# State-space layer: chunks of 4 tokens become chunks of 8, with column strips on TensorE and taps spread in memory

## The chip, the cores and the metric

The program runs on one core of one Trainium2 chip. The metric is the device time of one execution in microseconds; of several runs the median is given. The engines named in the rows are PE (matrix products), DVE, ACT and POOL (operations on vectors), and SP, which here issues the transfers.

## What is computed

A trunk of two layers for 256 tokens, with 16 meta tokens put ahead (272 columns) and 2048 channels. Layer 0 mixes by attention and a short convolution, layer 1 by a diagonal complex state-space layer with a gated output (GLU). Each is followed by a SwiGLU feed-forward net, with norms between. The part that matters here is the state-space mixer: 128 groups of 16 channels, each group with 64 complex states.

```python
def s5_mixer(u, a_re, a_im, log_step, b_re, b_im, c_re, c_im, d_skip, w_glu1, w_glu2):
    ...
    lb_re = mag * jnp.cos(ang)
    lb_im = mag * jnp.sin(ang)
    ...
    bu_re = jnp.einsum('blgh,gph->blgp', ug, bb_re)
    bu_im = jnp.einsum('blgh,gph->blgp', ug, bb_im)
    ...
    _, _, x_re, x_im = lax.associative_scan(_complex_affine_combine, (a_r, a_i, bu_re, bu_im), axis=1)
    y = (jnp.einsum('blgp,ghp->blgh', x_re, c_re.astype(f32))
         - jnp.einsum('blgp,ghp->blgh', x_im, c_im.astype(f32)))
    y = y.reshape(Bsz, L, D_MODEL) + d_skip.astype(f32) * uf
    g = jax.nn.gelu(y).astype(u.dtype)
    return (g @ w_glu1) * jax.nn.sigmoid(g @ w_glu2)
```

## The kernel before

Activations lie with channels on partitions: 16 tiles of 128 channels (`KT`) by 272 tokens. Every large product is made of three (high by high, high by low, low by high part, L296 to L298, L754). A weight chunk (`raw`, 384 to 512 KB) comes by DMA into one of four buffers, ACT makes its high part (L101), DVE its low part (L108), then PE uses both. SP issues all transfers in the order of the program.

The state-space layer works in chunks of `T` tokens. From the state at the start of a chunk the outputs of all its tokens follow by a product with C times powers of the transition; the effect of inputs on outputs inside the chunk is a triangular product with kernel taps. So the scan runs over `NC` = 272/`T` columns only. The matrices for this depend on parameters alone. `par_tile(k)` computes them for channel tile k on POOL and DVE, with transposes and a few small products on PE (`kmat`, L1029, is the one for the taps), and stores them to memory (`scr`). It is cut into ticks; the function `tick()` runs one after each weight chunk, so that all 16 tiles are made beside the feed-forward net of layer 0 (about 515 to 1205 us). Small tables of parameters are set up in the same way a little earlier.

After that net the stage proper follows. The input is turned by a round trip through memory (`write_u`, `read_u`, L1241 to L1247), so that the tokens of a chunk lie on partitions, and scaled by `r_u`. Then `s5_step(i)` (L1276) runs for i = -1 to 17. Each step issues operations for several tiles, as the table `stages` says, with a lag in steps: loads, `f_u` (scale, DVE, tile m), `f_c` (drive x of the states, PE, L1145), `f_mod` (rotation on DVE into rc and rs_, then z on POOL), `f_scan` (two DVE scans, L1171, rotation back, then xp on POOL), `f_y` (output product, PE, L1185 and L1188, and an ACT copy yn), `f_yt` (four PE transposes, L1197, and an ACT copy yy, then the first GELU steps), `f_g1` (POOL), `f_g2` and `f_g3` (DVE and ACT; the results xh and xl are the high and low part of the GLU's input). Lines 811 and 814 are the helpers `tt` and `stt` that record most DVE operations. Steps 18 to 23 run in the ticks of the first GLU block, whose first product starts at 1439.09 us.

## Time and profile before

| what | value |
| --- | --- |
| median of 3 runs | 2399.0 us (2397.54 to 2399.22) |
| the profiled execution's own time | 2399.63 us |
| its span, first to last instruction | 2397.9 us |
| PE busy | 2341.3 us (98%) |
| DVE busy | 1431.2 us (60%) |
| ACT busy | 1062.3 us (44%) |
| POOL busy | 708.5 us (30%) |
| mean granted TensorE clock | 0.991 |
| DMA, mean over the span | 187 GB/s |

Busy shares are means over stages with different limits, so a stage has to be read by itself: in windows of busy time, in the chain of waits (the work that ended last, followed back), and in the timeline of an engine. One matmul call on 4-byte floats is two records in the trace; the calls that work on the high and low parts are one. Durations of neighbouring operations overlap a little, so the time from start to start is what counts.

### The profile page before, as it was taken

The page shows a single profiled execution, that of the slowest core. Times are in us where ns is not written, and L with a number is a line of the kernel's source. Part 1 is how long each engine was busy: PE and PEld are TensorE (multiplying, and loading weights), DVE is VectorE, ACT ScalarE, POOL GpSimd, SP SyncE. Part 2 cuts the span into 40 slices and gives each one's busy share as a digit, 9 for nine tenths or more (in the row PEclk, how much of TensorE's full clock was granted, in tenths as well). Part 3 has the DMA queues.
Part 4 walks back from the last instruction along what each step waited for, and adds up shares of the span by engine and source line. Part 5 has one row for each costly group of instructions (what it writes and reads, how often), then busy time and mean ns, then how long its engine had stood idle before and what let it go on. Part 6 is the DMA issues. An engine that isn't in the chain of part 4 may idle for free.

```text
span 2397.9 us, 45436 instructions
## 1 busy us (share of the span) xinstructions
PE 2341.3 (98%) x18006; PEld 2251.5 (94%) x18006; DVE 1431.2 (60%) x1977; ACT 1062.3 (44%) x1613; POOL 708.5 (30%) x1214
## 2 busy tenths in 40 slices
PE   8999999999999999999999879999999999999998
PEld 7999999999999999999999769998998899989996
DVE  6555555677654576656554896457564455645665
ACT  5434344554343344334344555446444444433443
POOL 2000001248775878567501462105000000000001
PEclk9999999999999999999999899999999999999999
DMA  6555555457876788777755755555666566656664
GB/s 173 142 158 144 157 149 170 138 173 192 222 220 196 204 229 213 216 202 205 212 188 175 263 208 165 185 170 150 198 186 205 183 183 178 204 185 185 189 189 158
DMA packets 392537, 447.35 MB, mean 187 GB/s; under 512 B 75476, under 2 KB 324084, under 8 KB 392180
## 3 DMA queue, kind: packets, MB, share of 16 engines
q1 hardware_dynamic: 392096, 444.37, 63.3%
q8 instruction: 141, 2.31, 0.4%
q14 instruction: 72, 0.59, 0.1%
q10 hardware_dynamic: 228, 0.08, 0.0%
HBM read 413.50 MB, written 30.87 MB: 185 GB/s over the span
## 4 chain that ended last, share of the span: by engine, by line
PE 88%; DVE 7%; POOL 2%; ACT 1%; issue 1%; DMA 1%; SPq 0%; DVEq 0%; POOLq 0%; ACTq 0%
PE mm L296 23%; PE mm L298 23%; PE mm L297 22%; PE mm L754 5%; PE mm L1379 3%; PE mm L1380 3%; PE mm L1378 3%; DVE v L1171 1%; DVE wlo L108 1%; PE mm L1029 1%; PE mm L1017 1%; DVE rc L811 0%; DVE m L811 0%; DVE yq L814 0%; DVE hn L709 0%
## 5 line engine op out<-in xcount | busy, mean ns | idle before, releaser
L108 DVE TENSOR_TENSOR wlo<-raw,whi 128x768 fp32r<-128x768 f32 (+2 forms) x891 | 938.8, 1065 | 508.5 <-ACT whi L101 503.9
L101 ACT CAST whi<-raw 128x768 fp32r<-128x768 f32 (+2 forms) x891 | 777.5, 887 | 791.0 <-PE mm L297 460.8
L296 PE MATMUL mm<-xh,whi 128*128 128x272 f32 (+1 forms) x3712 | 1067.1, 287 | 0.8 <-DVE m L811 0.6
L298 PE MATMUL mm<-xh,wlo 128*128 128x272 f32 (+1 forms) x3712 | 1063.5, 287 | 4.0 <-DVE wlo L108 3.5
L297 PE MATMUL mm<-xl,whi 128*128 128x272 f32 (+1 forms) x3712 | 1057.1, 285 | 2.2 <-DVE xl L718 2.1
L298 PEld LDWEIGHTS mm<-xh,wlo 128*128 128x128 f32 x3712 | 700.6, 189 | 7.7 <-DVE wlo L108 7.6
L296 PEld LDWEIGHTS mm<-xh,whi 128*128 128x128 f32 x3712 | 702.3, 189 | 4.2 <-ACT sq L308 0.8
L297 PEld LDWEIGHTS mm<-xl,whi 128*128 128x128 f32 x3712 | 700.7, 189 | 3.2 <-DVE xl L718 3.2
L296 PE MATMUL mm<-ah,whi 128*128 128x272 f32 x944 | 273.9, 290 | 0.5 <-ACT m L677 0.5
L298 PE MATMUL mm<-ah,wlo 128*128 128x272 f32 x944 | 273.3, 289 | 0.0
L297 PE MATMUL mm<-al,whi 128*128 128x272 f32 x944 | 271.6, 288 | 0.0
L811 POOL TENSOR_TENSOR m<-m,gb 128x512 f32<-128x512 f32 x8 | 12.1, 1513 | 709.2 <-ACT mm L1392 692.9
L296 PEld LDWEIGHTS mm<-ah,whi 128*128 128x128 f32 x944 | 177.6, 188 | 1.1 <-ACT m L677 0.7
L298 PEld LDWEIGHTS mm<-ah,wlo 128*128 128x128 f32 x944 | 177.9, 188 | 0.1
L297 PEld LDWEIGHTS mm<-al,whi 128*128 128x128 f32 x944 | 177.9, 188 | 0.0
L313 POOL TENSOR_TENSOR sqacc<-sqacc,sq 128x272 f32<-128x272 f32 (+1 forms) x81 | 84.7, 1045 | 242.5 <-ACT sq L308 240.7
L1379 PE MATMUL mm<-wlo,ah 128*128 128x512 f32 x352 | 137.2, 390 | 1.0 <-DVE wlo L108 1.0
L1378 PE MATMUL mm<-whi,ah 128*128 128x512 f32 x352 | 137.8, 392 | 0.0
L1380 PE MATMUL mm<-whi,al 128*128 128x512 f32 x352 | 137.1, 390 | 0.0
L763 DVE TENSOR_TENSOR gs<-mm,r 128x272 f32<-128x272 f32 (+1 forms) x88 | 38.2, 434 | 113.2 <-PE mm L298 113.2
L581 POOL TENSOR_TENSOR z<-c,x 128x272 f32<-128x272 f32 x8 | 6.3, 785 | 289.7 <-DVE x L574 192.8
L1379 PEld LDWEIGHTS mm<-wlo,ah 128*128 128x128 f32 x352 | 66.1, 188 | 15.3 <-DVE wlo L108 1.8
(424 smaller groups left out, 2503.8 us busy)
## 6 DMA issues: line engine op xcount, KB each, us to landing
raw<-in_ffn_w_gate_dram SPq DMA_DIRECT2D x224, 384.0 KB, 3.8
raw<-in_ffn_w_up_dram SPq DMA_DIRECT2D x224, 384.0 KB, 3.9
raw<-in_ffn_w_down_dram SPq DMA_DIRECT2D x168, 512.0 KB, 4.6
raw<-in_ab_w_in_dram SPq DMA_DIRECT2D x90, 512.0 KB, 3.9
raw<-in_s_w_glu_dram SPq DMA_DIRECT2D x64, 384.0 KB, 3.6
raw<-in_ab_w_o_dram SPq DMA_DIRECT2D x32, 512.0 KB, 4.2
w<-scr SPq DMA_DIRECT2D x16, 768.0 KB, 4.3
scr<-xw SPq DMA_DIRECT2D x16, 512.0 KB, 5.0
```

Of the source, the lines that this page charges most:

```text
L101: self.nc.scalar.copy(hi[:, :n], self.raw[i][:, :n])
L108: self.nc.vector.tensor_tensor(lo[:, :n], raw[:, :n], hi[:, :n].bitcast(F32), op=ALU.subtract)
L296: nc.tensor.matmul(ps, hi, bh, start=first, stop=False)
L297: nc.tensor.matmul(ps, hi, bl, start=False, stop=False)
L298: nc.tensor.matmul(ps, lo, bh, start=False, stop=last)
L313: eng.tensor_tensor(self.acc[:, :self.cols], self.acc[:, :self.cols], sq[:, :self.cols], op=ALU.add)
L754: nc.tensor.matmul(pss[o], w[:, k, o * P:(o + 1) * P], xx[:, k, :cols], start=(k == 0 and w is hi and xx is xh), stop=False)
L763: nc.vector.tensor_tensor(gs[:, o, :cols], pss[o], r["r"][:, :cols], op=ALU.mult)
L1017: nc.tensor.transpose(pt[:, j * P:(j + 1) * P], wide["b"][:, i, j].rearrange("p s h -> p (s h)"), ident)
L1378: nc.tensor.matmul(pss[a], ah[:, kt, ts_], hi[:, k], start=(kt == 0), stop=False)
L1379: nc.tensor.matmul(pss[a], ah[:, kt, ts_], lo[:, k], start=False, stop=False)
L1380: nc.tensor.matmul(pss[a], al[:, kt, ts_], hi[:, k], start=False, stop=(kt == kts - 1))
```

## The change

`T` goes from 4 to 8, so a scan has 34 columns per state row where it had 68. The powers are made by doubling: complex products with the first, second and fourth power for each of B and C; the last of C runs on DVE in two ticks. The matrices are no longer widened with zeros for pairs of groups: B's and C's products use half of the partitions, and PE is addressed in column strips (`f_c` two strips of 64, `f_y` and `kmat` four of 32, by where the output's partitions start). `f_y` delivers channels in blocks of 32 that one DVE transpose turns, straight from PSUM; the transposes on PE and both ACT copies are gone, and xh and xl are written with a stride of 8. The triangular matrix of taps is made in memory: `store_k` and `zeros` write the 16 x 15 x 128 block `taps`, one tile later `spread_k` copies it eight times into `toep`, whose rows are read back with a skew as `kt`, in one transfer per tile. `f_load1` is merged into `f_load`, and the loads of `w2` and `kt` go out two steps ahead.

```diff
-T = 4
+T = 8
...
+    ZB = 2 * T - 1
+    KL = (ZB + T - 1) * P
+    taps = [dram.tile([16, ZB, P], F32, name=f"taps{k}") for k in range(KT)]
+    toep = [dram.tile([T, 16 * KL + P], F32, name=f"toep{k}") for k in range(KT)]
...
-        def bpow(n):
-            cmul([bc[:, i, :, T - 1 - n] for i in range(2)], [bc[:, i, :, T - n] for i in range(2)], s["lbr"][:, q], s["lbi"][:, q], ct)
...
+        def bpow(e):
+
+            bc, n = wide["b"], 1 << e
+            ar, ai = powers(e)
+            cmul(steps(bc, T - 2 * n, n), steps(bc, T - n, n), ar[:, q], ai[:, q])
...
         def kmat():
-            pt = d["pk"] = bank()
+
+            d["pk"] = []
+            for g in range(2):
+                pt = bank()
+                d["pk"].append(pt)
+                r = slice(64 * g, 64 * g + 64)
+                for i in range(2):
+                    for j in range(4):
+                        nc.tensor.matmul(pt[32 * j:32 * j + 32, :P], wide["b"][r, i, j, T - 2:].rearrange("p n h -> p (n h)"),
+                                         wide["c"][r, i, j, :T].rearrange("p n h -> p (n h)"), start=(i == 0), stop=(i == 1))
...
+        def store_k():
             for j in range(4):
-                for i in range(2):
-                    nc.tensor.matmul(pt[:32, j * 64:(j + 1) * 64], wide["b"][:, i, j, T - 1], cc[:, i, j, :T].rearrange("p n h -> p (n h)"), start=(i == 0), stop=(i == 1))
-
-        def k_first():
-
-            v = d["pk"][:32, :256].rearrange("p (qn h) -> p qn h", h=16)
-            o = kz[:32].rearrange("p q n (g h) -> p (q n) g h", g=2)
-            sh = [32, 4 * T, 2, 16]
-            tt(o, v.unsqueeze(2).to_broadcast(sh), evn[:32].unsqueeze(1).unsqueeze(3).to_broadcast(sh), M_)
-            tt(kz[:32, :, 0], kz[:32, :, 0], d["dd"], A_)
-
-        def ke(t):
-            V.tensor_copy(kz[32 * t:32 * t + 32, :, t:, :], kz[:32, :, :T - t, :])
+                nc.sync.dma_start(out=taps[k][:, T - 1:, 32 * j:32 * j + 32], in_=kk[32 * j + 16:32 * j + 32].rearrange("p n g h -> p n (g h)"))
+
+        def zeros():
+            nc.sync.dma_start(out=taps[k][:, :T - 1], in_=kz.unsqueeze(1).to_broadcast([16, T - 1, P]))
+
+        def spread_k():
+            v = toep[k][:, :16 * KL].rearrange("t (h n) -> t h n", h=16)[:, :, :ZB * P]
+            nc.sync.dma_start(out=v, in_=taps[k].rearrange("h b n -> h (b n)").unsqueeze(0).to_broadcast([T, 16, ZB * P]))
...
         def store():
             w = scr[k]
-            nc.sync.dma_start(out=w[:, CW0:KW0], in_=wide["c"].rearrange("p i q n h -> p (i q n h)"))
-            nc.sync.dma_start(out=w[:, KW0:], in_=kz.rearrange("p q t h -> p (q t h)"))
-            for i in range(2):
-                nc.sync.dma_start(out=w[:, EW0 + NT * i:EW0 + NT * (i + 1)].rearrange("p (q c) -> p q c", q=4), in_=d["e"][:, i, :, :NC])
-
-        loads[k] = load
+            nc.sync.dma_start(out=w[:, EW0:CW0], in_=d["e"].rearrange("p i q c -> p (i q c)"))
+            nc.sync.dma_start(out=w[:, CW0:], in_=wide["c"].rearrange("p i q n h -> p (i q n h)"))
...
+            [lambda: cpow(1, 1, 2), zeros], [lambda: etab(0), lambda: k and spreads[k - 1]()], [lambda: xw(0), lambda: etab(1)], [lambda: xe(0), lambda: cpow(2, 1, 4, V, 0)],
+            [lambda: xw(1), lambda: cpow(2, 1, 4, V, 1)], [lambda: xe(1)],
+            [kmat, store_x], [], [k_first], [store_k, store]]
...
-        w = sp.tile([P, EW0], F32, tag="w", name="w", bufs=3)
-        nc.sync.dma_start(out=w, in_=scr[k][:, :EW0])
+        w = sp.tile([P, CW0], F32, tag="w", name="w", bufs=5)
+        nc.sync.dma_start(out=w, in_=scr[k][:, :CW0])
...
     def f_load2(k):
-        w = sp.tile([P, SCR - CW0], F32, tag="w2", name="w2", bufs=2)
+        w = sp.tile([P, SCR - CW0], F32, tag="w2", name="w2", bufs=3)
         nc.sync.dma_start(out=w, in_=scr[k][:, CW0:])
+        kt = td[k]["kt"] = sp.tile([P, T, 8, 16], F32, tag="kt", name="kt", bufs=3)
+        v = toep[k].rearrange("t n -> (t n)")[:P * KL].rearrange("(r n) -> r n", r=P)
+        nc.sync.dma_start(out=kt.rearrange("r t j h -> r (t j h)"), in_=v[:, (T - 1) * P:ZB * P])
...
         for i in range(2):
             for j in range(4):
-                c0 = XW0 + 512 * i + P * j
-                nc.tensor.matmul(d["x"][:, i, j * NC:(j + 1) * NC], d["w"][:, c0:c0 + P], d["U"][:, j], start=True, stop=True)
+                for g in range(2):
+                    c0, o = XW0 + 512 * i + P * j + 64 * g, i * QC + j * NC
+                    nc.tensor.matmul(d["x"][64 * g:64 * g + 64, o:o + NC], d["w"][:, c0:c0 + 64], d["U"][:, 2 * j + g], start=True, stop=True)
...
     def f_y(k):
         d = td[k]
-        ps = sps.tile([P, 512], F32, tag="y", name="y")
-        for j in range(4):
-            o = ps[:NC - CM, j * P:(j + 1) * P]
-            w = d["w2"]
-            nc.tensor.matmul(o, d["U"][:, j, CM:], w[:, KW0 - CW0 + P * j:KW0 - CW0 + P * (j + 1)], start=True, stop=False)
+        ps = d["ps"] = sps.tile([P, 2, 512], F32, tag="y", name="y")
+        wv = d["w2"].rearrange("p (a n) -> p a n", a=8)[:, :, 16:]
+        kv = d["kt"].rearrange("p t j h -> p j t h")
+        for g in range(2):
+            for j in range(4):
+                nc.tensor.matmul(ps[32 * j:32 * j + 32, g, :P].rearrange("c (t h) -> c t h", t=T), d["U"][:, 2 * j + g, CM:], kv[:, 2 * j + g], start=True, stop=False)
+        for g in range(2):
+            r = slice(64 * g, 64 * g + 64)
             for i in range(2):
-                c0 = 512 * i + P * j
-                nc.tensor.matmul(o, d["xp"][:, i, j, CM:], w[:, c0:c0 + P], start=False, stop=(i == 1))
-        d["yn"] = sp.tile([NC - CM, T, 4, 32], F32, tag="yn", name="yn", bufs=1)
-        nc.scalar.copy(d["yn"].rearrange("c t q h -> c q t h"), ps[:NC - CM].rearrange("c (q t h) -> c q t h", q=4, t=T))
+                for j in range(4):
+                    nc.tensor.matmul(ps[32 * j:32 * j + 32, g, :P], d["xp"][r, i, j, CM:], wv[r, 4 * i + j], start=False, stop=(i == 1))
     def f_yt(k):
         d = td[k]
-        pt = sps.tile([P, 512], F32, tag="yt", name="yt")
-        n = NC - CM
-        for t in range(T):
-            nc.tensor.transpose(pt[:, t * n:(t + 1) * n], d["yn"][:, t].rearrange("c q h -> c (q h)"), ident[:n, :n])
         y = d["y"] = sp.tile([P, NREAL], F32, tag="yy", name="yy")
-        nc.scalar.copy(y.rearrange("p (c t) -> p t c", t=T), pt[:, :NREAL].rearrange("p (t c) -> p t c", t=T))
+        V.transpose(y.rearrange("p (t g h) -> p t g h", t=T, g=2), d["ps"][:, :, :P].rearrange("p g (t h) -> p t g h", t=T))
...
-        stt(xl[:, k, :NREAL], d["q"], 0.5, xh[:, k, :NREAL].bitcast(F32), M_, S_)
+        stt(by_step(xl[:, k, :NREAL]), d["q"].rearrange("p (t c) -> p t c", t=T), 0.5, by_step(xh[:, k, :NREAL].bitcast(F32)), M_, S_)
...
+        v = ub[g].rearrange("(s h) (j n) -> j h s n", s=T, j=8)
+        for j in range(8):
+            nc.sync.dma_start(out=v[j], in_=hs[g][16 * j:16 * j + 16].rearrange("h s k c -> h s (k c)"))
...
+            for t in range(4):
                 p = slice(32 * t, 32 * t + 32)
-                nc.scalar.activation(r_u[p], xt[p, 0, :NT].rearrange("p (c s) -> p c s", s=T)[:, :, t], AF.Sqrt, bias=eps_t[p])
+                v = xt[p, :NT].rearrange("p (c s) -> p c s", s=T)
+                nc.scalar.activation(r_o[p], v[:, :, 2 * t], AF.Copy, scale=evn[p, 0:1])
+                stt(r_u[p], v[:, :, 2 * t + 1], evn[p, 1:2], r_o[p], M_, A_)
+            nc.scalar.activation(r_u, r_u, AF.Sqrt, bias=eps_t)
...
-    stages = [(f_load2, 3), (f_load, -1), (f_load1, 0), (f_mod, 2), (f_c, 1), (f_g3, 8), (f_g2, 7), (f_u, -1),
+    stages = [(f_load2, 2), (f_load, -1), (f_mod, 2), (f_c, 1), (f_g3, 8), (f_g2, 7), (f_u, -1),
               (f_g1, 6), (f_scan, 3), (f_yt, 5), (f_y, 4)]
-    ahead = {f_load: 3, f_load1: 3, f_load2: 1}
+    ahead = {f_load: 3, f_load2: 2}
```

On SP beside the net of layer 0, around the stores of one tile (`scr` and `toep` are in memory, `raw` is a weight chunk), before:
```order
L95 DMA raw_7213<-in_ffn_w_up_dram 128x2x384
L1068 DMA scr_4494<-wide_c 128x1024
L1069 DMA scr_4494<-kz 128x512
L1071 DMA scr_4494<-e 128x4x68 x2
L95 DMA raw_7241<-in_ffn_w_gate_dram 128x2x384
L1044 DMA es<-etabs 128x2x68
```
and after, at the same place of that tile:
```order
L96 DMA raw_7282<-in_ffn_w_up_dram 128x2x384
L1069 DMA taps_4510<-kk 16x8x32 x4
L1104 DMA scr_4494<-e 128x320
L1105 DMA scr_4494<-cc 128x1152
L96 DMA raw_7312<-in_ffn_w_gate_dram 128x2x384
L1080 DMA es<-etabs 128x2x52
```
with the copy of the tile before it, earlier in the same tile's ticks:
```order
L1072 DMA taps_4510<-kz 16x7x128
L96 DMA raw_7037<-in_ffn_w_up_dram 128x2x384
L1076 DMA toep_4525<-taps_4509 8x16x1920
L96 DMA raw_7068<-in_ffn_w_gate_dram 128x2x384
L96 DMA raw_7102<-in_ffn_w_up_dram 128x2x384
```
The stores of wide_c, kz and e became four small ones of taps, one of e and one of cc, and a memory-to-memory transfer of 8x16x1920 stands among the weight chunks.

On PE in a steady step of the state-space stage, before:
```order
L1145 MATMUL x<-m,w 128x68 x8
L1197 MATMUL yt<-ident,yn 128x64 x4
L1185 MATMUL y<-w_16791,m 64x128
L1188 MATMUL y<-w_16791,xp 64x128 x2
L1185 MATMUL y<-w_16791,m 64x128
L1188 MATMUL y<-w_16791,xp 64x128 x2
L1185 MATMUL y<-w_16791,m 64x128
L1188 MATMUL y<-w_16791,xp 64x128 x2
L1185 MATMUL y<-w_16791,m 64x128
L1188 MATMUL y<-w_16791,xp 64x128 x2
```
and after, two steps:
```order
L1178 MATMUL x<-m,w 64x34 x16
L1219 MATMUL y<-kt,m 32x128 x8
L1224 MATMUL y<-w_16550,xp 32x128 x16
L1178 MATMUL x<-m,w 64x34 x16
L1219 MATMUL y<-kt,m 32x128 x8
L1224 MATMUL y<-w_16627,xp 32x128 x16
```
The four transposes are gone; the calls on xp no longer alternate with those on m, each is a call of 32 or 64 columns of weights, and there are twice as many.

On DVE in a steady step, before:
```order
L1171 SCALAR_TENSOR_TENSOR v<-d_16244,z 128x272 x2
L811 TENSOR_TENSOR rc<-v,w_16598 128x544
L811 TENSOR_TENSOR rs__16827<-v,w_16598 128x544
L811 TENSOR_TENSOR rc<-x,w_16728 128x544
L811 TENSOR_TENSOR rs__16865<-x,w_16728 128x544
L814 SCALAR_TENSOR_TENSOR xl<-yq,xh 128x256
L814 SCALAR_TENSOR_TENSOR yq<-yq,yy 128x256
L811 TENSOR_TENSOR m<-m,r_u 128x4x68
L1171 SCALAR_TENSOR_TENSOR v<-d_16245,z 128x272 x2
```
and after:
```order
L1204 SCALAR_TENSOR_TENSOR v<-d_16125,z 128x136 x2
L822 TENSOR_TENSOR rc<-v,w 128x272
L822 TENSOR_TENSOR rs__16830<-v,w 128x272
L1230 STREAM_TRANSPOSE yy<-y 128x256
L822 TENSOR_TENSOR rc<-x,w 128x272
L822 TENSOR_TENSOR rs__16873<-x,w 128x272
L825 SCALAR_TENSOR_TENSOR xl<-yq,xh 128x8x32
L825 SCALAR_TENSOR_TENSOR yq<-yq,yy 128x256
L822 TENSOR_TENSOR m<-m,r_u 128x8x34
L1204 SCALAR_TENSOR_TENSOR v<-d_16126,z 128x136 x2
```
The scans and rotations have half of their columns, and the transpose yy<-y stands between the two pairs of rotations.

## Rows read from the trace of the kernel before

**Rows 1.** Busy time by stretch: PE, PEld, DVE, ACT, POOL, clock, DMA share, GB/s
```profile
515.00:1205.00 690.00, 689.11 (x5603) 684.60 (x5602) 418.88 (x549) 276.37 (x347) 476.06 (x959) 1.00 0.75 209
...
1314.00:1336.00 22.00, 16.00 (x56) 8.81 (x56) 13.11 (x27) 17.40 (x40) 6.65 (x11) 0.83 0.84 269
1336.00:1442.00 106.00, 89.97 (x662) 80.81 (x662) 99.72 (x132) 52.46 (x143) 61.87 (x73) 0.91 0.66 229
```

**Rows 2.** The same view, one step of the state-space stage
```profile
1383.46:1390.40 6.94, 5.59 (x47) 4.72 (x46) 6.84 (x11) 3.73 (x10) 4.11 (x6) 1.00 0.64 230
```

**Rows 3.** Chain of waits, 1330 to 1445 us: start, length, engine, tile, line
```profile
1336.51 7.11 PE x L1145 x32
...
1345.35 2.35 DVE v L1171 x2
...
1369.07 2.31 DVE v L1171 x2
...
1437.89 2.32 DVE v L1171 x2
```

**Rows 4.** Timeline of DVE, same step: start, length, operation, shapes, count
```profile
1383.38 1.86 DVE L1171 TENSOR_TENSOR_SCAN v<-d,z 128x272 f32<-128x272 f32 x2
1385.35 0.73 DVE L811 TENSOR_TENSOR rc<-v,w 128x544 f32<-128x544 f32 x1
...
1386.62 0.72 DVE L811 TENSOR_TENSOR rc<-x,w 128x544 f32<-128x544 f32 x1
...
1387.89 0.69 DVE L814 SCALAR_TENSOR_TENSOR xl<-yq,xh 128x256 fp32r<-128x256 f32 x1
1388.51 0.98 DVE L814 SCALAR_TENSOR_TENSOR yq<-yq,yy 128x256 f32<-128x256 f32 x1
1389.41 0.99 DVE L811 TENSOR_TENSOR m<-m,r_u 128x272 f32<-128x272 f32 x1
```

**Rows 5.** All scans of line 1171: shortest, median, longest (ns), first and last start
```profile
L1171 DVE TENSOR_TENSOR_SCAN v<-d,z x32: 693/1228/1280, 1345.3 to 1444.0; 128x272 f32<-128x272 f32 x32
```

**Rows 6.** Timeline of DVE at the start of the stage
```profile
1341.50 0.43 DVE L811 TENSOR_TENSOR m<-m,r_u 128x272 f32<-128x272 f32 x1
```

**Rows 7.** Groups on ACT by shape, 1356 to 1420 us: busy us, mean ns
```profile
L1199 ACT COPY yy<-yt 128x256 f32<-128x256 f32 x10 | 6.1, 611 | 0.8 <-PE yt L1197 0.8
...
L1201 ACT ACTIVATE yq<-yy 128x256 f32<-128x256 f32 x10 | 4.2, 418 | 0.3
```

**Rows 8.** Timeline of PE, the step of rows 4
```profile
1383.74 2.00 PE L1145 MATMUL x<-m,w 128*128 128x68 f32 x16
1386.53 0.46 PE L1197 MATMUL yt<-ident,yn 64*128 64x64 f32 x4 [0.79 <-ACT yn L1190]
...
1388.84 0.60 PE L1188 MATMUL y<-w,xp 128*64 128x128 f32 x4
1389.28 0.38 PE L1185 MATMUL y<-w,m 128*64 128x128 f32 x2
```

**Rows 9.** Timeline of PE in the attention of layer 0
```profile
95.86 0.68 PE L549 MATMUL aux<-pt,vn 128*64 128x272 f32 x4
```

**Rows 10.** Busy time by stretch, two us while the loads fill the queue
```profile
1317.00:1319.00 2.00, 0.81 (x6) 0.71 (x6) 1.05 (x3) 0.02 (x1) 0.00 (x0) 0.84 1.04 426
```

**Rows 11.** Timeline of SP (its DMA issues) at the start of the stage
```profile
1330.28 1.89 SPq L1244 DMA_DIRECT2D ub<-hs  x4
```

**Rows 12.** Timeline of PE around one kmat
```profile
637.76 1.08 PE L1029 MATMUL mm<-cc,wide_b 128*32 128x64 f32 x16
```

**Rows 13.** DMA issues of the page: operation, count, size, median us to landing
```profile
raw<-in_ffn_w_gate_dram SPq DMA_DIRECT2D x224, 384.0 KB, 3.8
...
scr<-e SPq DMA_DIRECT2D x32, 136.0 KB, 8.4
```

**Rows 14.** Chain of waits, 560 to 600 us
```profile
572.44 8.20 DMA raw<-in_ffn_w_gate_dram
```

**Rows 15.** Timeline of PE, 580.6 to 583 us: idle before and releaser in brackets
```profile
582.62 0.39 PE L298 MATMUL mm<-xh,wlo 128*128 128x272 f32 x1 [0.48 <-DVE wlo L108]
```

More of the change, by code (lines that the diff above doesn't have):

```diff
@@ L829, in par_load @@
         nc.sync.dma_start(out=ls, in_=s5_log_step[0].rearrange("(q g) -> q g", g=2))
-        s["dn"], s["gd"] = an[:, 3, :32], an[:, 3, 32:64]
-        nc.sync.dma_start(out=s["dn"], in_=s5_d[0].rearrange("(q h) -> q h", h=32))
+        dn = s["dn"] = an[:32, 3]
+        V.memset(dn, 0.0)
+        V.memset(kz, 0.0)
+        for t, src in ((dn.rearrange("r (q x) -> r q x", q=4), s5_d[0]), (gd, norm_g[1, 0])):
+            v = src.rearrange("(k q g h) -> g k q h", q=4, g=2, h=16)
+            for g in range(2):
+                nc.sync.dma_start(out=t[16 * g:16 * g + 16, :, 16:], in_=v[g])
         V.memset(half_pi, 0.5 * math.pi)
@@ L937, in trunk, with cmul, steps, powers @@
         lambda: tt(s["cim"], s["t2"], s["t0"], M_))
-    def cmul(o, v, ar, ai, t):
-        arb = ar.unsqueeze(2).to_broadcast([P, 4, 16])
-        aib = ai.unsqueeze(2).to_broadcast([P, 4, 16])
-        t0, t1, t2, t3 = t
-        G.tensor_tensor(t0, v[0], arb, op=M_)
-        G.tensor_tensor(t1, v[1], aib, op=M_)
-        G.tensor_tensor(t2, v[0], aib, op=M_)
-        G.tensor_tensor(t3, v[1], arb, op=M_)
-        G.tensor_tensor(o[0], t0, t1, op=S_)
-        G.tensor_tensor(o[1], t2, t3, op=A_)
-    ct = [pr.tile([P, 4, 16], F32, name=f"ct{i}") for i in range(4)]
-    def open_wide():
-        for n, tag in (("b", "bw"), ("c", "cw")):
-            wide[n] = pr.tile([P, 2, 4, T, 32], F32, tag=tag, name=f"wide_{n}")
-            G.memset(wide[n], 0.0)
-    loaded, loads = {}, {}
+    ct = [pr.tile([P, 2, 4, 16 * T // 2], F32, name=f"ct{i}") for i in range(2)]
+    def cmul(o, v, ar, ai, conj=False, eng=None, part=None):
+        n = v.shape[3]
+        a, b = (t[:, :, :, :n] for t in ct)
+        if part in (None, 0):
+            for t, f in ((a, ar), (b, ai)):
+                tt(t, v, f.unsqueeze(1).unsqueeze(3).to_broadcast([P, 2, 4, n]), M_, eng or G)
+        if part in (None, 1):
+            tt(o[:, 0], a[:, 0], b[:, 1], A_ if conj else S_, eng or G)
+            tt(o[:, 1], a[:, 1], b[:, 0], S_ if conj else A_, eng or G)
+    def open_wide():
+        wide["b"] = pr.tile([P, 2, 4, T, 16], F32, tag="bw", name="bc")
+        wide["c"] = pr.tile([P, 2, 4, T + 1, 16], F32, tag="cw", name="cc")
+    def steps(t, a, n):
+        return t.rearrange("p i q n h -> p i q (n h)")[:, :, :, 16 * a:16 * (a + n)]
+    def powers(n):
+        return s["lbr l2r l4r".split()[n]], s["lbi l2i l4i".split()[n]]
+    loaded, loads, spreads = {}, {}, {}
     def par_tile(k):
@@ L978, in b_first @@
         def b_first():
-            d["dd"] = pr.tile([32, 4, 32], F32, name="dd")
-            G.tensor_tensor(d["dd"], ident[:32, :32].unsqueeze(1).to_broadcast([32, 4, 32]), dT[:, q].unsqueeze(2).to_broadcast([32, 4, 32]), op=M_)
+            bc = wide["b"]
             G.tensor_tensor(bx, bx, gk.unsqueeze(1).to_broadcast([P, 2, 4, 16]), op=M_)
-            cmul([bc[:, i, :, T - 1] for i in range(2)], [bx[:, i] for i in range(2)], s["cre"][:, q], s["cim"][:, q], ct)
+            cmul(steps(bc, T - 1, 1), bx, s["cre"][:, q], s["cim"][:, q])
         def c_t():
@@ L1233, in turn @@
             if k == 8:
[L1235 removed]
+                v = sp.tile([P, SCR - CW0], F32, tag="w2", name="hs", bufs=3)[:, :4 * NT]
                 hs[2] = v.rearrange("p (s k c) -> p s k c", s=T, k=4)
```

141 lines of the change are left out of this document (74 added, 67 removed).

## The prediction

> **What bounds the kernel now.** I read the busy windows by stretch first, then the chain of waits in the state-space stage, then one step of that stage on DVE and on PE. Beside the feed-forward net of layer 0, PE is busy 689.11 of 690 us [rows 1]: there only what PE itself executes, or a weight chunk that comes too late, moves the end. In the two stretches of the state-space stage PE is not full: 16.00 of 22 us, then 89.97 of 106 us, while DVE has 99.72 of the 106 [rows 1]. One step in steady state is 6.94 us, DVE 6.84, PE 5.59, ACT 3.73, POOL 4.11 [rows 2], and the chain names the DVE scan once per step [rows 3]. So DVE is the limit of a step, about 6.9 us sixteen times over, and the change halves most of what DVE does in a step. The profiled execution took 2399.63 us, the median of the three runs is 2399.0; I sum against the former and take the same difference from the latter.
>
> **The DVE step.** The chain gives the length: four early steps from 1345.35 to 1369.07, 5.93 us each (the GELU operations have not begun), then ten from 1369.07 to 1437.89, 6.88 us each [rows 3]. The ten consist of these, from start to start [rows 4]: two scans 1.97, four rotations of 128x544 at 0.64 (2.54), xl 0.62, yq 0.90, m 0.91 (0.99 less the 0.08 by which operations overlap). With 8 tokens in a chunk the scans go from 272 to 136 columns and the rotations from 544 to 272; xl, yq and m keep 256 and 272. New is one DVE transpose of 256 columns, which takes the place of an ACT copy, four PE transposes and a second ACT copy.
> - Scans: half, 1.0. A scan of 272 takes 693 ns at its quickest, 1228 in the median, so this is mostly time beside POOL [rows 5].
> - Rotations: 272 columns take 0.43 (m alone, [rows 6]) against 0.72 for 544 [rows 4]; the difference 0.29 is 272 columns, and with the same overlap it is 0.35 each, 1.4 in all.
> - yq, m, xl: 0.90 + 0.91 + 0.62 = 2.43 as they stand. m takes 0.43 undisturbed and 0.99 here; POOL's z and xp operations halve too, from about 4.1 to about 2.9 us a step, so up to 0.6 comes back. xl is now written with a stride of 8 floats. No DVE row shows that; the nearest are two ACT copies of 256 columns, 611 ns strided and 418 plain [rows 7]: 0 to +0.2.
> - Transpose: not in the trace. From below 0.35, a DVE operation of as many columns; from above 0.9, one of as many beside POOL [rows 4]. I take 0.4, because it reads PSUM like the rotation of x, which runs no slower than that of v.
> Sum 1.0 + 1.4 + 2.4 + 0.4 = 5.2, and 5.3 with a little for the stride; 4.7 to 5.9. Ten steps: 10 x (6.88 - 5.3) = **-15.8 us** (-21.8 to -9.8).
>
> **What is late next in a step.** PE: f_c (L1145) has 16 records in 2.00 us and f_y (L1185, L1188) 24 records of 128 columns at 0.11 [rows 8]. After, f_c has 32 records in two column strips and f_y 48 in four strips. That strips run side by side is shown by the attention of layer 0: L549, two strips of 64, puts four records of 272 columns into 0.68 us [rows 9], while 272 columns at 0.11 per 128 are 0.23, four in a row 0.93. Then f_y is six groups of two records, 1.3 to 1.5, f_c 1.0 to 2.0; together 3.5, below 5.3. ACT loses yn and keeps the rest, below 4. DMA: a tile's loads grow from 128 x 3104 floats (1.59 MB) to 128 x 3520 (1.80 MB). The queue moved 426 GB/s where it was full [rows 10], so 4.2 us; below 5.3, but not by much.
> f_y now has one PSUM tile that the DVE transpose must empty before the next f_y starts. Behind that wait on PE stands f_c of the next step, whose result DVE wants one step later; the transpose sits in mid-step and f_y takes 1.4, so some 3 us of slack cover it.
>
> **The ends of the stage.** The four early steps hold fewer DVE operations and more DMA, and PE runs at the half clock there; I take 5.4 for 5.93, **-2** (-4 to 0). Before them, f_c of the first two tiles holds the chain for 7.11 us [rows 3]; side by side it would be half, load-bound the same. Against it stand four small DVE operations in r_u (about +1), and 32 instead of 16 write_u issues: four took 1.89 us [rows 11], eight would take 3.8, about the 3.6 us between two groups, so they just keep up, and 1.1 MB more is loaded ahead of them, 2.6 us at 426 GB/s on a queue that is already busy. Net **-1** (-3 to +2). After the first GLU matmul, f_y of tiles 14 and 15 and the last transposes stand in PE's own row: 2.6 + 0.46 + a wait of 0.8 per tile [rows 8], against 1.4 after: two tiles, **-5** (-6 to -2).
>
> **Beside the feed-forward net of layer 0.** POOL does fewer and larger operations and DVE gains four per tile; neither bounds there. On PE only kmat (L1029) changes: 16 records in 1.08 us, about 1.0 that PE's matmuls wait [rows 12]; after, 32 records of 128 columns in four strips: 0.8 if all four overlap, 1.8 if they go in pairs. I take 0.8, by [rows 9]: 16 x -0.2 = **-3** (-3 to +13). The stores change shape: e was written in pieces of 272 bytes and took 8.4 us to land [rows 13], it is now one row of 1280 bytes; wide_c shrinks to 590 KB with cc, kz gives way to five small transfers, and 16 copies of 983 KB from memory to memory are added, one per tile. On average that is 0.85 MB more per 43 us, 20 GB/s over the 209 of that stretch [rows 1]. For the first tile a burst of stores once delayed a chunk to 8.20 us [rows 14], and PE waited for it, 0.48 us at the longest [rows 15]; **-0.5** (-2 to +1). In the setup, DVE gets eight more operations of 128x64, each below the 0.43 of 272 columns [rows 6] when undisturbed, in a stretch that DVE holds up: 0.25 each, **+2** (0 to +4).
>
> Sum: -15.8 - 2 - 1 - 5 - 3 - 0.5 + 2 = -25.3: 2399.6 to 2374.3, and from the median 2373.7. **Forecast 2374 us.** The terms' bounds are not all reached together; I count 2362 to 2388 for this case.
>
> **Rivals.**
> 1. The spread starves the weights (the other side). The copy toep<-taps has an outer dimension of 8. If that puts it on 8 of 16 engines, half of 426 GB/s moves 983 KB in 4.6 us, and in 9 if reading and writing share the engine. A weight chunk that needs all engines would land after 3.8 [rows 13] and 4.6, 8.4 together, or 13 us. The landing of 8.20 us cost PE 0.48 [rows 14, 15], so from about 8 on each us is one of PE; at 10 us PE loses 2 us sixteen times, +32: 2374 + 32 = **2406**. It decides from a landing of about 8.2 us; below that the ring of four chunks hides it. Against: the copy has 43 us until the next. The Trainium skill, "DMA: Bandwidth & Descriptors", Rules for kernel authors, says exactly that an outermost dimension of size c below 16, for instance a leading broadcast of c copies, confines the whole transfer to at most c engines; no row of the trace before shows a transfer of this shape. By that rule the 4.6 holds, without it 2.3 and nothing in the sum. Chance 0.11.
> 2. Loads become the bound of a step. In steady state the trace shows 230 GB/s [rows 2]. At 5.3 us the step needs 339. Were only 300 to be had, because SP issues late behind f_y, the step is 6.0 and the ten give -8.8: **2381**; at 270 GB/s 6.7: 2388. For: 0.64 share before. Against: 426 [rows 10]. Chance 0.13.
> 3. Strips don't overlap. f_y 48 x 0.11 = 5.3, f_c 2 to 4: about 8 us a step against 6.7 on average, 14 steps +18; kmat 3.5 for 1.0, +40: **about 2455**. It decides where f_y and f_c pass 6.9 us. Against: [rows 9]. Chance 0.03.
> 4. The change shortens DVE's work, but a latency across engines (f_u, f_c, rotation, POOL, scan, POOL, f_y, transpose) sets the step at 6.5 or more, so that it doesn't do what it says: -4 in the ten steps and the rest eaten by the start, **2392 to 2398**. Against: stages lag each other by a whole step each. Chance 0.06.
>
> **How the numbers follow.** Forecast 0.67, rivals 0.11, 0.13, 0.03, 0.06. About 0.2% (4.8 us) is what a measurement of this kernel tells from no change. Faster: 0.67 + 0.13 + 0.01 of the last = 0.81. Same: 0.04 of the last and 0.02 of the first = 0.06. Slower: 0.09 of the first, 0.03, 0.01 = 0.13. Range 2358 to 2396: it takes in the forecast and the second rival, and leaves out the first and third, half of the last and a tail of 0.04 below.
>
> **What would show it.** Right: scans start 5.3 us apart in steady state with DVE near full; the scans' group at about half its mean; the first GLU matmul some 20 us nearer to the first scan; f_y's records overlapping in PE's timeline; kmat near 0.8. Wrong: PE gaps after each toep copy with a chunk that lands late (rival 1), DVE idle behind w or kt (2), f_y above 4 us (3), DVE idle without any engine full (4), or a transpose of 1 us and more, which would move the step towards 5.9.

## The result

The changed kernel takes 2367.57 us (median of 4 runs, 2365.92 to 2368.95) against 2398.27 for the kernel before: a ratio of 0.9872, 95% interval 0.9855 to 0.9889. The forecast was 2374, so the direction was right and the gain, 30.7 us, about a fifth larger than the 25.3 that were summed. The profiled execution of the changed kernel took 2368.0 us with a span of 2366.2. (Of the two runs of the kernel with sixteen engines below one was disturbed, 2800.15 us at a mean granted clock of 0.743; the other is used.)

Where the time went, by starts of PE products in the two traces (us; the first column starts at the 29th product of the net of layer 0, at 513.96 before and 514.12 after; the stage runs from the net's last product to the first of the GLU):

| | net of layer 0 | stage | first 300 products of the GLU | from there to the last product |
| --- | --- | --- | --- | --- |
| before | 799.69 | 125.44 | 45.00 | 903.95 |
| after | 797.68 | 99.73 | 39.98 | 904.47 |
| difference | -2.01 | -25.71 | -5.02 | +0.52 |

The net's first product comes at 508.83 before and at 510.51 after; up to the 29th it is 5.13 us before and 3.61 after.

The first rows are the windows of busy time of the changed kernel, with the columns of [rows 1]; the last of them is one steady step and answers to [rows 2].

```profile
515.00:1205.00 690.00, 685.93 (x5874) 679.11 (x5873) 447.14 (x601) 274.89 (x350) 414.45 (x560) 1.00 0.72 227
1312.00:1334.00 22.00, 17.04 (x57) 9.74 (x56) 12.83 (x28) 16.33 (x37) 6.99 (x12) 0.77 0.89 280
1334.00:1411.50 77.50, 55.74 (x1184) 43.26 (x1184) 71.47 (x150) 41.91 (x121) 46.02 (x75) 0.57 0.97 356
1372.71:1377.64 4.93, 3.98 (x84) 3.04 (x84) 4.83 (x11) 2.87 (x9) 3.10 (x6) 0.50 0.99 376
```

A steady step lasts 4.93 us for 6.94, and DVE is still full in it, 4.83. Two things are new: the DMA share is 0.99, and the granted clock is 0.50, the lower level of 1.2 GHz, where a step before had 1.00. PE's busy 3.98 us is therefore work at the half clock. The net of layer 0 has lost some fullness: PE 685.93 of 690 us, 689.11 before [rows 1].

The DVE timeline of that step answers to [rows 4].

```profile
1372.63 1.29 DVE L1204 TENSOR_TENSOR_SCAN v<-d,z 128x136 f32<-128x136 f32 x2
1374.03 0.44 DVE L822 TENSOR_TENSOR rc<-v,w 128x272 f32<-128x272 f32 x1
1374.39 0.43 DVE L822 TENSOR_TENSOR rs__16910<-v,w 128x272 f32<-128x272 f32 x1
1374.74 0.44 DVE L1230 STREAM_TRANSPOSE yy<-y 128x256 f32<-128x256 f32 x1
1375.11 0.40 DVE L822 TENSOR_TENSOR rc<-x,w 128x272 f32<-128x272 f32 x1
...
1375.78 0.61 DVE L825 SCALAR_TENSOR_TENSOR xl<-yq,xh 128x256 fp32r<-128x256 f32 x1
1376.31 0.70 DVE L825 SCALAR_TENSOR_TENSOR yq<-yq,yy 128x256 f32<-128x256 f32 x1
1376.94 0.71 DVE L822 TENSOR_TENSOR m<-m,r_u 128x272 f32<-128x272 f32 x1
```

From start to start: scans 1.40, four rotations 1.39, transpose 0.37, xl 0.53, yq 0.63, m 0.63, in all 4.93. The chain of waits in the stage (start, length, engine, tile, line) answers to [rows 3].

```profile
1336.72 3.65 PE x L1178 x64
1341.54 1.20 DVE v L1204 x2
...
1356.01 1.46 DVE v L1204 x2
...
1406.67 1.22 DVE v L1204 x2
...
1409.45 1.08 PE y L1219 x16
```

Scan 0 is at 1341.54, scan 4 at 1356.01, scan 14 at 1406.67. The two tiles of f_c that held the chain for 7.11 us now hold it for 3.65. The ten steps from scan 4 to scan 14 are not all alike: the first lasts 6.80 us, since the drive x waits there for a load, and later ones 4.93 to 4.95, one 5.41, the last two 8.80 together. PE at f_c in the first of them:

```profile
1358.20 1.93 PE L1178 MATMUL x<-m,w 128*64 128x34 f32 x32 [2.20 <-DMA w<-scr]
```

### The profile page after: what moved, and what is told of

Its sections match the earlier page's. It is cut to its first block, busy times and chain, and to the rows that moved or that the text cites. A ratio compares the mean times of both kernels' runs of the same rounds, so it can differ in the third digit from the quotient of the medians.

```text
span 2366.2 us, 46781 instructions
## 1 busy us (share of the span) xinstructions
PE 2300.8 (97%) x18838; PEld 2204.6 (93%) x18838; DVE 1430.0 (60%) x2056; ACT 1043.9 (44%) x1582; POOL 622.4 (26%) x811
## 4 chain that ended last, share of the span: by engine, by line
PE 89%; DVE 7%; ACT 1%; POOL 1%; DMA 1%; issue 1%; SPq 0%; DVEq 0%; ACTq 0%; POOLq 0%
PE mm L297 23%; PE mm L299 23%; PE mm L298 23%; PE mm L755 5%; PE mm L1421 3%; PE mm L1422 3%; PE mm L1420 3%; DVE wlo L109 2%; DVE v L1204 1%; PE mm L1041 1%; POOL ct L822 0%; DVE xl L719 0%; PE mm L1058 0%; DVE hn L710 0%; DMA raw<-in_ffn_w_gate_dram 0%
## 5 line engine op out<-in xcount | busy, mean ns | idle before, releaser
L109 DVE TENSOR_TENSOR wlo<-raw,whi 128x768 fp32r<-128x768 f32 (+2 forms) x891 | 957.3, 1087 | 498.7 <-ACT whi L102 491.7
L822 POOL TENSOR_TENSOR bc<-ct,ct 128x64 f32<-128x64 f32 (+2 forms) x128 | 88.5, 712 | 89.6 <-PE mm L1058 85.7
```

What stands on the lines that cost most here:

```text
L109: self.nc.vector.tensor_tensor(lo[:, :n], raw[:, :n], hi[:, :n].bitcast(F32), op=ALU.subtract)
L822: (eng or V).tensor_tensor(o, a, b, op=op)
```

## The experiments

Nine edits of the changed kernel were made alone, on strips, loads, the copies, ticks, PSUM, the clock and POOL, and three sets were put together. "Net" and "stage" below are the columns of the table above. Kernels that are the same in the net differ there by up to 3.2 us from run to run (794.49 to 797.68), and in the stage by about 2, so single times within 3 us decide nothing here; rows do.

**Do column strips run side by side?** First f_y's calls were put in an order in which neighbours use the same strip.

```diff
-        for g in range(2):
-            for j in range(4):
+        for j in range(4):
+            for g in range(2):
...
```

> The calls of f_y are issued in another order, so that neighbouring calls use the same column strip; the same 24 calls, nothing left out. Theory (column strips side by side are what keeps PE below DVE): f_y of 48 records grows from 2.2 us at the half clock to about 5 at the full clock (48 x 0.11) or more, and with f_c at 1 to 2 us PE sets the step at 6 to 7 us instead of 4.94; ten steps cost +10 to +20 us and the end of the stage some more: 2380 to 2395 us. Rival (records of 32 columns are cheap by themselves, the order does not matter): f_y stays near 2.2 us, the step stays at 4.94, the time stays at 2367.

Measured: 2369.28 us. The two parts of f_y took 1.11 and 1.18 us at the half clock, 1.08 and 1.13 in the changed kernel. The theory's number was wrong, but the order proved to be no test of strips: records still start in groups of four within 50 ns, although neighbours in program order now name the same strip. That a call waits only for its own strip would explain it; the trace does not name the strip of a record, so this is not shown. So eight calls to one strip alone were added after each step.

```diff
...
+                for j in range(8):
+                    nc.tensor.matmul(wm[:32, :P].rearrange("c (t h) -> c t h", t=T), d["U"][:, j, CM:], kv[:, j], start=True, stop=True)
```

> After each step from step 4 on, eight calls like those of f_y on kt, but all to one column strip (the first 32 PSUM partitions of a place nobody reads), are added on PE; they measure the price without strips. Theory (different strips run side by side, calls of one strip one after the other): the 16 records take four times the 0.85 us that 16 records in four strips take from first to last group at the half clock, about 3.4 us (1.7 at the full clock). Rival (calls of 32 columns are quick by themselves): about 1.1 us as in f_y.

The timeline of PE in one step of that kernel: f_y on kt, f_y on xp, the added calls.

```profile
1374.62 0.65 PE L1219 MATMUL y<-kt,m 128*32 128x128 f32 x16 [0.76 <-DVE yy L1230]
1375.20 0.69 PE L1224 MATMUL y<-w,xp 64*32 64x128 f32 x32
1375.82 1.94 PE L1329 MATMUL wm<-kt,m 128*32 128x128 f32 x16
```

The same 16 records take 0.65 us in four strips and 1.94 in one (at the full clock, which the added work brought), 0.11 us from start to start. That is near the theory's 1.7, and rival 3 of the prediction is settled: without strips f_y's 48 records would take some 5.3 us by this spacing, more than a whole step now. With these calls on PE in each step, and its clock doubled, the steps stayed at 4.95 us (2367.59 us in all, one run): PE is not the bound.

**DVE or the loads?** The DMA share of 0.99 in a step left open which of the two sets its length. kt was loaded for tile 0 alone, so that the other 15 tiles use its taps.

```diff
...
+        if k == 0:
+            kt1.append(sp.tile([P, T, 8, 16], F32, tag="kt", name="kt", bufs=1))
...
+        td[k]["kt"] = kt1[0]
```

> The tap matrix kt is loaded for channel tile 0 alone and used for all 16; 15 of the 16 loads of 0.5 MB are left out (the outputs of the other tiles use the wrong taps). The DMA share of the state-space stage, 0.97 to 1.0, falls to about 0.7. Theory (DVE sets the steady step): steps stay at 4.94 us with DVE full, only the places where PE waits for w in the first steps get shorter, 1 to 4 us in all: 2363 to 2367 us. Rival (the loads set the step, DVE only keeps pace with them): steps fall below 4.7 us, and the stage loses 3 us or more in the ten steady steps besides: below 2362 us.

Its busy windows over two steps, and its chain:

```profile
1372.00:1382.00 10.00, 6.23 (x172) 4.89 (x170) 9.79 (x21) 5.81 (x17) 6.24 (x10) 0.84 0.78 265
```

```profile
1371.02 1.23 DVE v L1207 x2
1375.97 1.23 DVE v L1207 x2
1380.91 1.23 DVE v L1207 x2
```

The share fell to 0.78 and the steps stayed 4.94 to 4.95 us. DVE sets the steady step; the loads just fit. One step is the exception: from scan 4 to scan 5, the 6.80 us above, this kernel takes 5.17. There the loads set the length, as rival 2 of the prediction has it, and cost about 1.6 us once. 2366.47 us, stage 97.68.

**What do the copies into toep cost?** The copy was issued three times in a row, twice into memory that nobody reads.

```diff
+            for o in (toep[k], toex[2 * k + 0], toex[2 * k + 1]):
```

> The copy into toep is issued three times in a row, twice into memory that nobody reads; 2 MB more per channel tile. Theory (a chunk may land up to about 8 us late, beyond that PE pays each us): three copies hold 8 engines for some 25 us, chunks behind them land after 15 to 25 us, and PE waits 5 to 15 us in each of 16 tiles: 2450 to 2600 us. Rival (copies share the engines packet by packet with the chunks behind them, so those are only slowed): chunks land after 6 to 9 us, PE loses at most 1 us per tile: 2367 to 2385 us.

Measured 2517.9 us, ratio 1.0492 (1.0461 to 1.0522). A chunk behind the copies, in the chain of waits, and what PE waited for from 515 to 1240 us of a net that here lasts to about 1459 (total us, times, longest):

```profile
598.51 16.84 DMA raw<-in_ffn_w_gate_dram
615.45 0.83 ACT whi L102
616.28 0.49 ACT xw L1045
616.82 1.08 PE mm L1059 x16
```

```profile
PE mm L1059 <- ACT xw L1045: 68.3, 9, 8.9
PE mm L297 <- ACT whi L102: 16.9, 4, 5.1
PE mm L299 <- DVE wlo L109: 5.3, 6, 1.3
```

The chunk lands after 16.84 us. ACT waits for it in order, and behind it in ACT's row stands the copy xw out of the PSUM bank that kmat (L1059 here) needs; so PE stops inside kmat, for up to 8.9 us. The net takes 943.08 us, 145.4 more or about 9 for each of 16 copies, and 16.84 is 8.8 above 8: at this size the price is near what rival 1 of the prediction put, one for one beyond about 8 us, though part of it is products at the half clock behind the waits (granted 0.53 from 617.90 to 621.00). Does a single copy cost so little because of where it stands, and is its outer dimension of 8 the reason for its length? The order was changed so that the 16 channels are outermost.

```diff
-            v = toep[k][:, :16 * KL].rearrange("t (h n) -> t h n", h=16)[:, :, :ZB * P]
+            v = toep[k][:, :16 * KL].rearrange("t (h n) -> h t n", h=16)[:, :, :ZB * P]
...
```

> The copy into toep names the same bytes in another order, with the 16 channels outermost and the eight copies within; nothing else changes. Theory (the ring of four chunks hides a spread of 8 to 9 us): the net of layer 0 takes the same time within 0.5 us and the total stays at 2367, although chunks that were late behind the copy land about 1 to 2 us earlier. Rival (the copy on half of the engines costs PE waits for chunks): the net of layer 0 gets 2 us or more shorter, 2365 or less.

Measured 2367.06 us. The net took 794.39, 1.4 us below the mean of the seven kernels that are alike there; not resolved. The transfers changed as they should: in the changed kernel the copy's semaphore, which counts what has landed, rises in eight steps between 7.2 and 9.7 us after its issue (in 15 of 16 copies, after one rise at about 1.1 us), now in sixteen between 4.7 and 8.4, and the weight chunk right behind it lands after 4.5 to 8.6 us where it took 7.3 to 10.1. What PE waited for in the net (515 to 1205 us, and to 1240) in the changed kernel and with sixteen engines:

```profile
PE mm L299 <- DVE wlo L109: 2.8, 2, 1.7
PE mm L1058 <- ACT xw L1044: 1.3, 2, 0.8
```

```profile
PE mm L299 <- DVE wlo L109: 1.6, 2, 1.1
```

The waits in kmat are gone. From the product before kmat to the one behind it they cost the changed kernel 2.5 us in all; but the seven kernels that keep the copy on eight engines lose 0.0 to 2.5 there, 1.3 in the mean, so that one trace without a wait does not show the price by itself. It is small in any case, with chunks that land after up to 10.1 us. The 2.8 us are another thing: DVE's row in tile 0 of the changed kernel.

```profile
560.45 0.94 DVE L822 TENSOR_TENSOR ct<-cc,s_l4r 128x512 f32<-128x512 f32 x1 [3.21 <-POOL cc L822]
561.31 0.95 DVE L822 TENSOR_TENSOR ct<-cc,s_l4i 128x512 f32<-128x512 f32 x1
562.18 1.28 DVE L109 TENSOR_TENSOR wlo<-raw,whi 128x768 fp32r<-128x768 f32 x1
```

The product of powers that the change moved to DVE waits 3.21 us for POOL on this first tile, and a wlo stands behind it; the two gaps that follow on PE cost it some 3 us. Two empty ticks were put ahead of it, in tile 0 alone.

```diff
-            [lambda: cpow(1, 1, 2), zeros], [lambda: etab(0), lambda: k and spreads[k - 1]()], [lambda: xw(0), lambda: etab(1)], [lambda: xe(0), lambda: cpow(2, 1, 4, V, 0)],
+            [lambda: cpow(1, 1, 2), zeros], [lambda: etab(0), lambda: k and spreads[k - 1]()], [lambda: xw(0), lambda: etab(1)]] + [[]] * (2 * (k == 0)) + [[lambda: xe(0), lambda: cpow(2, 1, 4, V, 0)],
```

> Two empty ticks stand ahead of the DVE products of powers of channel tile 0, so that POOL has their input ready; all later tiles come two ticks later. Theory (in tile 0 DVE waits 3.2 us for POOL with a wlo behind it, and PE pays 1.95 and 1.37 us in two gaps near 562 and 566): both gaps vanish, the net of layer 0 is 2 to 3 us shorter, about 2365. Rival (the gaps come from late weight chunks there): they stay, the time stays at 2367.

Measured 2397.66 us, ratio 0.9993 (0.9982 to 1.0004): the two gaps vanished, and all of the change's gain with them. The chain in a later tile, and PE's timeline there:

```profile
642.33 8.34 DMA raw<-in_ffn_w_gate_dram
650.67 0.02 issue
650.69 0.04 ACTq L102
650.73 0.04 issue
650.77 0.83 ACT whi L102
651.60 0.49 ACT xw L1044
```

```profile
649.25 0.64 PE L1058 MATMUL mm<-cc,bc 64*32 64x128 f32 x16
652.14 1.07 PE L1058 MATMUL mm<-cc,bc 64*32 64x128 f32 x16 [2.25 <-ACT xw L1044]
```

All later tiles stood two weight chunks later, and a chunk behind the copy landed after 8.34 us, no later than in the changed kernel, but just where kmat needed ACT. PE waited 15.7 us for xw in nine tiles, and after such a wait its clock fell: the window 652.00 to 656.50 was granted 0.50. The net takes 825.35, 27.7 us more than in the changed kernel; 19.7 of these are longer stretches from the product before kmat to the one behind it and 7.2 are products at the half clock's spacing. With both edits:

> The two empty ticks in tile 0, and the copy into toep with the 16 channels outermost. Two ticks alone made 2397.7: chunks behind the copy landed after 8.3 us and PE waited about 2 us in most tiles. Theory (it is the copy's eight engines that are at fault, and the two ticks only moved it to a place with less in reserve): with sixteen engines the copy takes about half, no wait of 2 us is left, the gaps near 562 us stay away, and the net of layer 0 is 3 us shorter than after: 2363 to 2365. Rival (the shift itself is at fault, products of parameters that collide with other work): it stays above 2385.

Measured 2377.09 us. The net came down from 825.35 to 805.19, so the copy on eight engines, at this place, was most of it; 7.5 us stay against the changed kernel's 797.68 and 9.4 against the mean of the seven. Around kmat PE still loses 6.2 us, and chunks for the low parts come later too (PE waited 2.8 us for wlo in seven places). The theory held for most of the cause and not for the number; that the rest belongs to the shift of the later tiles is tried in the last set.

**What does the end of the stage wait for?** From scan 14 to the first GLU product it is 4.86 us, 1.20 before. PE's timeline of the changed kernel there:

```profile
1409.45 1.08 PE L1219 MATMUL y<-kt,m 128*32 128x128 f32 x16 [2.13 <-DVE yy L1230]
1410.47 1.13 PE L1224 MATMUL y<-w,xp 64*32 64x128 f32 x32
1411.53 0.58 PE L297 MATMUL mm<-xh,whi 128*128 128x256 f32 x1
1411.91 0.41 PE L298 MATMUL mm<-xl,whi 128*128 128x256 f32 x1
```

f_y of tile 13 waits for the transpose of tile 12, then runs at the half clock. A second PSUM place for y:

```diff
+        ps = d["ps"] = sps.tile([P, 2, 512], F32, tag="y", name="y") if k % 2 or k == KT - 2 else spx.tile([P, 2, 512], F32, tag="y2", name="y2", bufs=1)
```

> The PSUM tile that f_y writes alternates between two places, so that f_y no longer waits for the DVE transpose of the tile before (only tiles 14 and 15 still do). Theory (the wait costs nothing in steady steps, but at the end of the stage f_y of tiles 12 and 13 and with them the first GLU product wait for it): steady steps stay at 4.94 us, the time from scan 14 (1406.67) to the first GLU product, 4.86 us after, falls by 1.5 to 3 us; the total by 1 to 3 us: 2364.5 to 2367. Rival (the end is set by POOL's xp of tile 13 and by PE at the half clock, not by this wait): at most 0.5 us earlier.

Measured 2367.32 us. f_y of tile 13 starts at 1405.51 instead of 1409.45, but now the first GLU product waits:

```profile
1405.51 1.08 PE L1219 MATMUL y<-kt,m 128*32 128x128 f32 x16 [2.39 <-DVE yy L1230]
...
1410.14 0.55 PE L297 MATMUL mm<-xh,whi 128*128 128x256 f32 x1 [2.48 <-DVE yy L1230]
```

Its PSUM banks are those of the second place, so it waits for the same transpose. Part of the wait moved there, but not all: the first GLU product starts 2.85 us behind scan 14 (1407.29) instead of 4.86, as the theory said, because f_y of tile 13 is done by then. The stage of 98.11 against 99.73 and the total do not resolve this from the spread. Then the clock: six products of 128x128 that nobody reads after each step.

```diff
...
+        if i >= 4:
+            for _ in range(6):
+                nc.tensor.matmul(wm[:, :P], mean_w, ones_w[:, :P], start=True, stop=True)
```

> From step 4 on, six products of 128x128 by 128 columns whose result nobody reads are added on PE after each step. Theory (PE has the half clock in the stage because it is idle part of each step, and this costs only at the end, where f_y and the first GLU products run at half clock): the granted clock in 1365 to 1411 us rises from 0.5 towards 1.0, steady steps stay at 4.94 us, and the end gains 1 to 3 us: 2364 to 2366. Rival (added PE work delays f_c and f_y, or the clock stays at half): the clock stays near 0.5 and the steps grow by up to 1 us, 2367 to 2378.

Its windows for two steps:

```profile
1372.71:1382.58 9.87, 7.67 (x193) 6.42 (x184) 9.66 (x21) 5.71 (x17) 6.22 (x11) 1.00 1.01 392
```

The clock is 1.00 and a step is 4.94 us still: the half clock costs a steady step nothing. 2367.61 us; the first 300 products of the GLU are 0.8 us shorter (39.20), and the products added after the last step stood in front of the GLU for 1.6.

**POOL beside DVE.** The product of f_g1 went from POOL to DVE.

```diff
-        G.tensor_tensor(d["q"], d["q"], d["y"], op=M_)
+        V.tensor_tensor(d["q"], d["q"], d["y"], op=M_)
```

> The product of f_g1 goes from POOL (0.93 us in a step) to DVE; nothing else. Theory (DVE operations beside POOL take 0.6 to 0.7 instead of 0.4 us, and the scans beside this product pay about 0.4 us): DVE gains 0.35 to 0.45 and loses 0.4 to 0.5 of contention, the step stays within 0.15 of 4.94, scans go from 1.23 to about 0.85 a pair; total 2366 to 2369. Rival (no contention, the scans are as long as they are): the step grows by 0.4 to 5.3, total 2371.

```profile
1374.50 0.41 DVE L1240 TENSOR_TENSOR yq<-yq,yy 128x256 f32<-128x256 f32 x1
1374.84 0.76 DVE L1204 TENSOR_TENSOR_SCAN v<-d,z 128x136 f32<-128x136 f32 x2
```

2364.79 us. DVE got a product of 0.34 us from start to start, and its two scans fell from 1.29 to 0.76: the step is 4.73 (transpose to transpose, 1371.68 to 1376.41). DVE, the bound, got an operation more and its step got shorter, because the scans no longer lie beside a POOL operation: one scan takes 0.41 us where POOL is idle and 0.71 (median) beside it, in the changed kernel too.

**Together.** A further set had the two ticks, sixteen engines, the six products only after steps 4 to 14, and in steps 16 and 17 the transpose ahead of the scans:

```diff
-        for f, lag in stages:
+        for f, lag in stages if i < KT else sorted(stages, key=lambda x: [f_load2, f_load, f_mod, f_c, f_g3, f_g2, f_u, f_g1, f_yt, f_scan, f_y].index(x[0])):
...
+        if 4 <= i < KT - 1:
```

> Both edits of the run before, six unread products on PE after steps 4 to 14 that hold the clock, and in steps 16 and 17 the DVE transpose ahead of the scans, so that f_y of tile 13 starts earlier. Theory: 3 us less beside the net of layer 0, 2 to 4 us at the end of the stage, where the first GLU product starts some 2.7 us after scan 14 instead of 4.9: 2360 to 2363. Rival (the end is held by the weight chunks of the GLU or by POOL, the net's waits come back elsewhere): 2364 to 2368.

2375.91 us, some 13 above the theory's upper end: the first GLU product comes 2.2 us behind scan 14, as hoped, and the stage takes 97.09, but the net 806.07, as in the kernel with two ticks and sixteen engines. In the last set tile 0 starts two ticks earlier besides, which leaves every later tile where the change had put it, and f_g1's product is on DVE.

```diff
-    queues[1].extend([[]] * BL)
+    queues[1].extend([[]] * (BL - 2))
```

> All that helped, together: the copy into toep with the 16 channels outermost; tile 0 starts two ticks earlier and has the two empty ticks, so that the later tiles stand where they stood in the changed kernel; the product of f_g1 on DVE; six unread products on PE after steps 4 to 14; in steps 16 and 17 the DVE transpose ahead of the scans. Theory (the shift of all later tiles cost the 8 to 10 us that two ticks and sixteen engines still lost; the rest adds up): net of layer 0 from 797.7 to 791.5 to 793.5, stage from 99.7 to 94 to 96, total 2357 to 2361. Rival (the sixteen-engine copy or the earlier start, not the shift, is at fault): net above 800, total above 2368.

2360.17 us, ratio to the kernel before 0.9842 (0.9828 to 0.9855). The net takes 792.24 and PE is busy 690.00 of the 690 us from 515 to 1205; the stage takes 95.36. The rival fell: in the net this kernel differs from the one with two ticks and sixteen engines only by the earlier start, so the shift of the later tiles was the rest.

```profile
515.00:1205.00 690.00, 690.00 (x5918) 684.09 (x5917) 450.29 (x608) 279.10 (x353) 410.49 (x560) 1.00 0.73 229
```

## Why the prediction was right

By its own terms, predicted and measured (us, one trace against the other):

| term | predicted | measured | from |
| --- | --- | --- | --- |
| ten steady steps | -15.8 | -18.2 | 68.82 to 50.66 between scans 4 and 14 |
| four early steps | -2 | -9.2 | 23.72 to 14.47 between scans 0 and 4 |
| up to scan 0 | -1 | -2.0 | 31.70 to 29.74 from the net's last product |
| scan 14 to the GLU | 0 | +3.7 | 1.20 to 4.86 |
| f_y within the GLU | -5 | -5.0 | first 300 products |
| net: kmat | -3 | -6 | 16 x (0.84 - 1.23), start to start of the products around it, without waits |
| net: stores, DVE | -0.5 | +4 | net -2.0 less kmat |
| setup | +2 | +1.7 | 508.83 to 510.51, first product of the net |
| first 28 products of the net | 0 | -1.5 | 5.13 to 3.61 |
| after the first 300 products | 0 | +0.5 | to the last product |

The sum of the terms, -25.3, came within 6 us of the measured gain, and that is in part luck: the early steps gave 7 us more than was taken, the end of the stage took 4 back that was taken at nothing, and kmat and the stores were both off, in opposite directions.

- **The bound.** DVE was the limit of a step and still is, and halving its columns gave the gain: confirmed by the rows of the step and by the kernel with fewer loads. PE's 3.5 us came out at 4.0, since a steady step now runs at the half clock, which was not foreseen; it cost such a step nothing.
- **The DVE step, 5.3 against 4.94 (5.07 in the mean of the ten, with the one that waited for loads).** Rotations (1.4 and 1.39) and transpose (0.4 and 0.37) came out as summed. Two mistakes partly cancelled. The scans did not halve (1.97 to 1.40, for 1.0), since they now lie beside POOL's product of f_g1; this is what its move to DVE showed. And xl, yq and m gave back 0.64 (2.43 to 1.79), all of the "up to 0.6" that the sum left out. In the step the stride of 8 does not show (xl 0.61 us, 0.69 before); where POOL is idle it does, at the end of the stage, with 0.68 to 0.72 us against 0.42 before.
- **The early steps, the largest error.** The prediction took 5.4 for 5.93 because of the loads and the half clock. But the trace before had DVE busy 5.50 of 5.53 us in the first of them and 5.82 of 5.92, 6.00 of 6.10 and 6.07 of 6.17 in the others, where the clock was 0.86 to 1.00, so DVE was the bound there too, and without the GELU operations nearly all of its work halves. The loads did fill the queue, 414 to 419 GB/s at a share of 1.02 to 1.03 in the second to fourth, and delivered until scan 4. PE reads as full in both rows below, but in the first early step of the changed kernel PE is busy 1.20 of 3.27 us and DVE 3.24. The rows of one step:

```profile
1345.35:1350.88 5.53, 5.53 (x27) 5.41 (x27) 5.50 (x8) 1.08 (x4) 3.47 (x5) 0.50 0.99 385
```

```profile
1344.81:1348.16 3.35, 3.35 (x74) 2.48 (x74) 3.25 (x8) 0.96 (x4) 2.08 (x5) 0.50 1.02 419
```

- **The added wait.** "Some 3 us of slack cover it" held in steady steps and not at the end, where no next step stands between: f_y of tile 13 waited 2.13 us for DVE, and what follows ran at the half clock: 3.7 us. The term was missing; the second place for y gave 2.0 of it back.
- **The net.** kmat in strips gained twice what was taken, and moving a product to DVE cost what the prediction had denied ("neither bounds there"): in tile 0 it waited for POOL with a wlo behind it, some 3 us of the 4; the other part is the 2.5 us around kmat behind the copy, less 1.4 us of gaps that the net had before. A queue position, not a load, was the price. The setup came out as forecast, +1.7 to the first product. The 1.5 us that the next 28 products gave back are luck: those before ran in part at the half clock (0.67 granted from 508.83 to 514.00, 1.00 after), and kernels with the same setup show both, 3.6 and 5.1 us.
- **Rival 1** was right about the mechanism: an outermost dimension below 16 confines a transfer to at most that many engines, says the Trainium skill, "DMA: Bandwidth & Descriptors", Rules for kernel authors. The runs agree: the copy's semaphore rose in eight steps and with 16 outermost in sixteen, and the chunk behind the first copy landed after 8.3 us, where the rival summed 8.4. Its threshold of 8.2 us was not a fixed one: in the changed kernel chunks behind the copy landed after 7.3 to 10.1 us and PE lost 2.5 us around kmat; two ticks later they landed after 8.1 to 10.4 and PE lost 22. It did not decide because in the changed kernel a chunk behind the copy was not needed just then, which the prediction had not worked out; two ticks of shift were enough to cost 30 us, so this too was luck.
- **Rival 2** came within a hair: in a steady step the share is 0.99, and the loads fit; in the step from scan 4 to scan 5 they did not, and PE waited 2.20 us for w. **Rival 3** fell by the one-strip rows. **Rival 4** fell: DVE is busy 4.83 of the 4.93 us of a step.

What stays open: how the 7.5 to 9.4 us of a shift of two ticks with sixteen engines divide between the chunks and the shorter reserve; and the extra 0.5 us behind the GLU's first 300 products, a stretch in which kernels that are alike there differ by up to 0.8.
